# An mLSTM and band-attention trunk on one core: the values of all heads first, one loop of heads with seven products on 7 of 8 depth pairs, weight sums on GpSimd

## The chip, the core and the metric

The kernel runs on one core of a Trainium2 chip. TensorE (PE) multiplies, VectorE (DVE) and ScalarE (ACT) work on tiles, GpSimd (POOL) can add tiles too, and SyncE (SP) issues the DMAs. The metric is the device time of one execution in microseconds, as the median of several.

## The reference

Two layers run on x of 512 tokens by 2048 channels, in float32. The first is an mLSTM with 8 heads, the second a band attention with 16 heads over a shared K and V. Each layer is normalised, modulated by a projection of `c` (adaLN) and gated. The time goes into the large products:

```python
proj = h @ w_in                      # 512x2048 @ 2048x16400: q, k (8 x 256 each), v, o, z (8 x 512 each), gates
qk = silu(causal_conv(proj[..., :A_V0]))
ht = rmsnorm(mlstm_chunkwise(q, k, v, li, lf))
y = sigmoid(o) * ht * silu(z)
x = x + gate0 * rmsnorm(y @ w_out)   # 512x4096 @ 4096x2048
kv = hkv @ kv_w                      # 512x2048 @ 2048x4096, shared K and V
qz = h2 @ b_w_in                     # 512x2048 @ 2048x4096: queries and gate
out = x + gate1 * rmsnorm((attention(q, k, v) * silu(z)) @ b_w_out)
shift, scale, gate = split(silu(c) @ ada_w[l] + ada_b[l])   # 2048 -> 6144 for each layer, 4096 for K and V
```

## The kernel before

**Products in three passes.** Each float32 operand is split into a high part (a cast on ScalarE, line 181) and a low part (a subtraction on VectorE, line 182); `mm3` issues high x high, high x low and low x high on TensorE (line 223). The names `wr`, `wh` and `wl` are a weight as loaded, its high and its low part. `h` is the modulated input of a layer, in 16 depth tiles of 128 channels by 512 tokens.

**Eight or seven products.** A unit is two depth tiles by two output tiles of 128 columns by 512 tokens. In the plain form it takes four triples over 512 tokens, which count as eight of 256. `proj_s` computes some units in Strassen's manner, with seven triples over 256 tokens, into four PSUM tiles D, C, A and B; this needs four sums of the inputs (`h1s`, kept in SBUF) and three sums of the weights. VectorE makes the sums of the weights (`ws`, lines 206 to 208), and they are split in their turn (`wsh`, `wsl`). `HEAD_PAIRS = 5` of the 8 units of a pair of output tiles are done so in heads 5 to 7, `RAMP = [4, 5, 5, 5]` in the o and z pairs of head 4, none in heads 0 to 3, and `ATT_PAIRS = 7` of 8 in the queries of the attention.

**Stages.** The start makes `h1` block by block while it multiplies the rows that are ready: q, k, o and z of head 0 and q, k of head 1. Then heads 0 to 7 run in a loop: q and k with their convolution (line 529), the values in `proj_b` (`ps_v`), the scores between them, o and z, the weighted values, the normalisation, and the head's result to DRAM (`ysc`). Then come a_w_out (tiles `y`), the shared values and keys, the 16 attention heads, and b_w_out.

**The columns of adaLN.** The projection of `c` is done on VectorE: rows of the transposed weights are loaded (`ada`, 128x1024, 256 loads) and multiplied and summed into columns of `mod` (line 381). The first 64 loads belong to the start; `background(n)` issues the others in heads 0 to 4 and sums those that came before, held in program order.

**Order.** The tile scheduler orders each engine's instructions by priority; weights are prefetched under a high priority (`AHEAD = 300`). SP issues nearly all DMAs in one queue, and each waits there for its buffer. Raw weights have two buffers of 128x1024 and one more from a spare pool in the start, in heads 0 to 4 and in a_w_out.

Of the kernel before, what the change touches and what calls it, by code (L numbers as in the profile page):

```python
# [33 lines left out]
RAW_BUFS = 2  # L34
# [3 lines left out]
LEAD = [0, P, V0 // 2, V0 // 2 + P, O0, O0 + P]  # L38
LATER = [O0 + 2 * P, O0 + 3 * P] + [Z0 + i * P for i in range(4)]
LATER += [DK, DK + P, V0 // 2 + DK, V0 // 2 + DK + P]  # L40


KEY_PAIRS = [6, 7, 8, 8, 8, 8, 8, 8]
HEAD_PAIRS = 5
RAMP = [4, 5, 5, 5]
HALF = NH // 2
ATT_PAIRS = 7


def pair_pieces(f, merged=False):  # L50


    sk, nk = list(range(f)), list(range(f, KT // 2))
    n = len(nk)
    assert n <= f
    out = [([[a]], [b]) for a, b in zip(sk, nk)]
    return out + [([sk[i : i + 2]] if merged else [[k] for k in sk[i : i + 2]], []) for i in range(n, f, 2)]


def stream():  # L60
# [3 lines left out]
    def add(mat, kts, cs):  # L64
        out.append((mat, [(k, c, n) for k in kts for c, n in cs]))

    def tile_a(mat, col, kts=KT):
        for k in range(0, kts, 8):
            add(mat, range(k, k + 8), [(col, P)])

    def tile_b(mat, col, kts=KT):
        for k in range(0, kts, 2):
            add(mat, [k, k + 1], [(col, 512)])

    def tile_s(mat, c1, c2, f, merged=False):
        for sk, nk in pair_pieces(f, merged):
            blocks = [(2 * k + i, c, P) for ks in sk for i, c in ((0, c1), (0, c2), (1, c2), (1, c1)) for k in ks]
            out.append((mat, blocks + [(2 * k + i, c, P) for k in nk for i in range(2) for c in (c1, c2)]))

    for k0, k1 in BLOCKS:  # L80
        for k in range(k0, k1):
            add("a_w_in", [k], [(c, P) for c in LEAD])
        for c in LATER:
            add("a_w_in", range(k0, k1), [(c, P)])
    for h in range(NH):
        for c in (h * DK, V0 // 2 + h * DK):
            if 1 < h <= HALF:
                tile_a("a_w_in", c)
                tile_a("a_w_in", c + P)
            elif h > HALF:  # L90
                tile_s("a_w_in", c, c + P, HEAD_PAIRS)
        tile_b("a_w_in", V0 + h * DV)
        if h >= HALF:
            for i in range(4):
# [38 lines left out]
def hybrid_trunk(ctx, tc, xT, xN, c, adaT, cols, wst, wg, ext, kc, out):  # L133
# [131 lines left out]
    def proj_s(mat, xs, ss, f, z1, z2, name, pl, bufs, at={}, merged=False):  # L265
# [6 lines left out]
        for i, (sk, nk) in enumerate(pieces):  # L272
# [35 lines left out]
            if i:  # L308
                eight()
# [309 lines left out]
    for h in range(NH):  # L619
# [62 lines left out]
        if h:  # L682
            so = []
# [480 lines left out]
```

## Time and profile before

| | |
|---|---|
| median of 3 runs | 2831.57 us (2830.79 to 2834.91) |
| the profiled execution | 2835.43 us |
| its span, first to last instruction | 2833.7 us |
| TensorE busy | 2790.5 us, 98% of the span |
| VectorE, ScalarE busy | 2073.8 us (73%), 1337.3 us (47%) |
| moved by DMA | 524.61 MB, 185 GB/s in the mean |

All shares are of the profiled execution. A busy time counts an engine as busy from an instruction's start to its end; TensorE's matmuls overlap, so the cost of one is read from the distance between the starts of two. In a row by group stand the busy time of the group, the mean duration in ns, and the engine's idle time before its instructions with what ended it.

### The profile page before, as it was taken

What the parts mean: (1) busy time and instruction counts of PE and PEld (TensorE: products, weight loads), DVE (VectorE), ACT (ScalarE), POOL (GpSimd) and SP (SyncE); (2) the same over time, 40 slices, a digit from 0 to 9 for tenths busy, and PEclk for the clock granted to TensorE, in tenths of its full rate; (3) what the DMA queues carried; (4) which work ended last, traced back from release to release, by engine and by line L of the source; (5) the groups of instructions that cost most, each with busy time, mean ns of one, the idle gap of its engine ahead of it and who ended that gap; (6) DMA issues with size and microseconds to landing.
All of it is one profiled execution on the core that took longest, in us unless ns stands there. A gap on an engine that the chain in (4) does not pass through costs nothing.

```text
span 2833.7 us, 40698 instructions
## 1 busy us (share of the span) xinstructions
PE 2790.5 (98%) x15308; PEld 2423.1 (86%) x15308; DVE 2073.8 (73%) x3680; ACT 1337.3 (47%) x2005; POOL 0.2 (0%) x4
## 2 busy tenths in 40 slices
PE   7999999999999999999999999999999999999998
PEld 5887888888888989989888888888998899999886
DVE  7986978778688776857766445567885798999625
ACT  4244524234234554545545444468434466666523
POOL 0000000000000000000000000000000000000000
PEclk9999999999999999999999999999999999999999
DMA  8875787868774333323324666788435533333535
GB/s 307 303 249 178 233 309 244 298 231 277 263 244 134 101 108 97 108 93 105 108 90 145 217 197 223 240 273 274 163 127 176 175 123 127 129 113 125 197 133 167
DMA packets 177117, 524.61 MB, mean 185 GB/s; under 512 B 18788, under 2 KB 36228, under 8 KB 176408
## 3 DMA queue, kind: packets, MB, share of 16 engines
q1 hardware_dynamic: 176920, 522.01, 55.4%
q8 instruction: 120, 1.97, 0.3%
q14 instruction: 77, 0.63, 0.1%
HBM read 488.33 MB, written 38.85 MB: 186 GB/s over the span
## 4 chain that ended last, share of the span: by engine, by line
PE 86%; DVE 6%; DMA 4%; ACT 2%; issue 2%; SPq 0%; DVEq 0%; ACTq 0%
PE ps_y L223 17%; PE ps_v L223 10%; PE ps_o L223 5%; PE ps_z L223 5%; PE ps_azo L223 4%; PE ps_qk L223 4%; PE ps_kv L223 4%; PE ps_az L223 3%; PE ps_bzo L223 3%; PE ps_l L223 3%; PE ps_cz L223 3%; PE ps_dz L223 2%; PE ps_bz L223 2%; PE ps_s L223 2%; PE ps_czo L223 2%; PE ps_dzo L223 2%
## 5 line engine op out<-in xcount | busy, mean ns | idle before, releaser
L181 ACT CAST wh<-wr 128x1024 fp32r<-128x1024 f32 (+3 forms) x586 | 585.3, 1000 | 843.9 <-PE ps_y L223 203.7
L182 DVE TENSOR_TENSOR wl<-wr,wh 128x1024 fp32r<-128x1024 f32 (+3 forms) x586 | 679.1, 1161 | 410.1 <-ACT wh L181 407.6
L223 PE MATMUL ps_y<-wh,y 128*128 128x512 f32 x1536 | 475.9, 390 | 0.1
L223 PEld LDWEIGHTS ps_y<-wh,y 128*128 128x128 f32 x1536 | 288.2, 188 | 60.0 <-ACT wh L181 0.3
L223 PE MATMUL ps_v<-wh,h 128*128 128x512 f32 x1024 | 321.6, 390 | 0.1
L223 PE MATMUL ps_y<-wl,y 128*128 128x512 f32 x768 | 299.3, 390 | 0.4 <-DVE wl L182 0.2
L181 ACT CAST wsh<-ws 128x384 fp32r<-128x384 f32 (+1 forms) x253 | 138.4, 547 | 315.4 <-issue 122.2
L223 PEld LDWEIGHTS ps_v<-wh,h 128*128 128x128 f32 x1024 | 192.3, 188 | 40.2 <-issue 1.0
L182 DVE TENSOR_TENSOR wsl<-ws,wsh 128x384 fp32r<-128x384 f32 (+1 forms) x253 | 151.7, 600 | 97.7 <-ACT wsh L181 96.3
L223 PE MATMUL ps_v<-wl,h 128*128 128x512 f32 x512 | 199.8, 390 | 0.0
L381 DVE CUSTOM_DVE_ANT_0 ada<-ada,scB,mod 128x1024 f32<-128x1024 f32 x128 | 164.1, 1282 | 24.5 <-DMA ada<-in_adaT 23.2
L381 DVE CUSTOM_DVE_ANT_0 ada<-ada,scB,cl 128x1024 f32<-128x1024 f32 x128 | 164.0, 1282 | 24.1 <-DMA ada<-in_adaT 23.7
L223 PEld LDWEIGHTS ps_y<-wl,y 128*128 128x128 f32 x768 | 144.3, 188 | 31.0 <-DVE wl L182 1.5
L223 PE MATMUL ps_kv<-wh,hkv 128*128 128x512 f32 x512 | 159.4, 391 | 0.0
L206 DVE TENSOR_TENSOR ws<-wr 128x256 f32<-128x256 f32 (+1 forms) x253 | 112.5, 453 | 37.6 <-DMA wr<-in_wst 34.5
L223 PE MATMUL ps_qk<-h,wh 128*128 128x512 f32 x384 | 119.1, 390 | 0.0
L223 PE MATMUL ps_o<-h,wh 128*128 128x512 f32 x384 | 118.2, 389 | 0.0
L223 PE MATMUL ps_z<-h,wh 128*128 128x512 f32 x384 | 118.1, 389 | 0.0
L223 PEld LDWEIGHTS ps_v<-wl,h 128*128 128x128 f32 x512 | 96.2, 188 | 19.7 <-issue 0.9
L223 PEld LDWEIGHTS ps_kv<-wh,hkv 128*128 128x128 f32 x512 | 95.7, 188 | 19.4
L223 PE MATMUL ps_l<-h,wh 128*128 128x512 f32 x320 | 99.6, 392 | 0.9 <-ACT wh L181 0.5
L223 PE MATMUL ps_kv<-wl,hkv 128*128 128x512 f32 x256 | 99.9, 390 | 0.4 <-DVE wl L182 0.4
(385 smaller groups left out, 5918.8 us busy)
## 6 DMA issues: line engine op xcount, KB each, us to landing
wr<-in_wst SPq DMA_DIRECT2D x520, 512.0 KB, 3.6
ada<-in_adaT SPq DMA_DIRECT2D x256, 512.0 KB, 5.8
xt<-nsc SPq DMA_DIRECT2D x46, 256.0 KB, 3.7
yr<-ysc SPq DMA_DIRECT2D x16, 512.0 KB, 4.0
wr<-in_wst SPq DMA_DIRECT2D x30, 256.0 KB, 4.4
wr<-in_wst SPq DMA_DIRECT2D x16, 384.0 KB, 5.0
bsc<-in_ext SPq DMA_DIRECT2D x16, 320.0 KB, 6.4
xt<-in_xT SPq DMA_DIRECT2D x4, 1024.0 KB, 7.0
```

The costliest lines, as they stand in the source:

```text
L181: nc.scalar.copy(hi, src)
L182: nc.vector.tensor_tensor(lo, src, hi.bitcast(F32), op=ALU.subtract)
L206: nc.vector.tensor_tensor(t[:, : 2 * w], r[:, w : 3 * w], r[:, : 2 * w], op=ALU.subtract)
L223: nc.tensor.matmul(ps, a, b, start=start, stop=stop)
L381: pin(nc.vector.tensor_tensor_reduce(at, at, scB[:, j * D // 2 : (j + 1) * D // 2], 1.0, mod[:, i : i + 1] if j else col(CB + i), ALU.mult ...
```

## The change

- The values of all heads come first. The start multiplies the values of heads 0 to 3 (`FIRST = 4`) in place of q, k, o and z; heads 4 to 7 follow in a loop of `proj_b`. All are kept in DRAM (`vrow`) as float32 and fetched and split again in each head.
- One loop of heads does q, k, o and z of every head with seven products on 7 of 8 units (`HEAD_PAIRS = 7`); the attention takes 8 of 8. A unit's input sums for the second token half overwrite the high and low parts that are no longer used, so seven units' sums fit.
- The three sums of the weights are on GpSimd, with signs changed so that all are additions. A seven-product piece is one load of 128x512; it is staged one piece ahead, and its products are ordered so that the three that need no sum come first.
- One pool for the weights: raw tiles of 128x512, four of them, and three (`ws`) that hold sums, and raw tiles of plain pieces where no sums are needed; in a_w_out and the first shared values (`plain`) only four.
- The columns of adaLN are spread otherwise: 56 loads of 128x1024 among the values of heads 4 to 6; 104 quarters (128x512) in the loop of heads; 104 in a_w_out and the first shared values; 32 loads of 128x1024 in b_w_out. Small parts: the attention's bias has one buffer, `gates_out` works on four columns at a time.

```diff
-HEAD_PAIRS = 5
-RAMP = [4, 5, 5, 5]
-ATT_PAIRS = 7
+FIRST = 4
+HALF_KV = 12
+TICKS = (2, 3, 5, 6)
+HEAD_TILES = 26
+HEAD_PAIRS = 7
+ATT_PAIRS = 8
+    return [0, *range(f, UNITS), *range(1, f)]
...
-            raw = (spare[0] if own else wp).tile([P, 1024], F32, tag="raw", name=f"wr{i}", bufs=1 if own else RAW_BUFS)[:, :n]
-                nc.vector.tensor_tensor(t[:, : 2 * w], r[:, w : 3 * w], r[:, : 2 * w], op=ALU.subtract)
-                nc.vector.tensor_tensor(r[:, w : 2 * w], t[:, w : 2 * w], r[:, :w], op=ALU.add)
-                nc.vector.tensor_tensor(t[:, 2 * w :], r[:, 3 * w :], r[:, w : 2 * w], op=ALU.subtract)
...
+        tag = "ws" if spare and not plain[0] and fresh[0] % 7 > 3 else "raw"
+        return wp.tile([P, 512], F32, tag=tag, name=name, bufs=3 if tag == "ws" else 4)
...
+            if not seven:
+                for c in range(0, n, 512):
+                    raw = rawtile(f"wr{i}_{c}", blocks[0][2] == 512)
+                    nc.sync.dma_start(raw, src[:, c : c + 512])
+                    cast = split(hi[:, c : c + 512], lo[:, c : c + 512], raw)
+            else:
+                raw = rawtile(f"wr{i}", False)
+                nc.sync.dma_start(raw, src)
+                t = wp.tile([P, 512], F32, tag="ws", name=f"ws{i}")
+                nc.gpsimd.tensor_tensor(
+                    t[:, : 2 * w].rearrange("p (a b) -> p a b", a=2), raw[:, : 2 * w].rearrange("p (a b) -> p a b", a=2),
+                    raw[:, 3 * w :].unsqueeze(1).to_broadcast([P, 2, w]), op=ALU.add,
+                )
+                nc.gpsimd.tensor_tensor(t[:, 2 * w : 3 * w], t[:, :w], raw[:, w : 2 * w], op=ALU.add)
+                nc.gpsimd.tensor_tensor(t[:, 3 * w :], t[:, 2 * w : 3 * w], raw[:, 2 * w : 3 * w], op=ALU.add)
+                cast = split(hi[:, : 3 * w], lo[:, : 3 * w], raw[:, : 3 * w])
+        staged.append((mat, hi, lo, t, cast))
+    def wpiece(want):
+        early = t is not None or AHEAD_ALL
+        if early and wpos[0] < len(order):
+            stage()
+        if t is not None:
+            with tc.high_priority(ahead[0]):
+                split(hi[:, 384:896], lo[:, 384:896], t)
...
+            raws = [(D, h0, 0, x0[:, :, h0]), (A, h0, 2, x1[:, :, h0]), (B, h0, 1, s[3])]
+            sums = [(D, h1_, 5, s[1]), (C, h0, 4, s[2]), (C, h1_, 3, s[0]), (A, h1_, 6, x1[:, :, h1_])]
+            steps = raws + sums
...
+    for h in range(FIRST, NH):
+        at = {k: lambda k=k: background((3, 2)[k // 2 % 2]) for k in range(0, KT, 2)}
+        proj_b("a_w_in", lambda k: h1[k], pv, at=at)
+                keep_rows(h, m, pv[m])
...
+        hooks = [{6: score[0]}, {1: score[1], 4: score[2], 7: score[3]}, {1: fetch[0], 3: fetch[1], 5: fetch[2], 7: fetch[3]}, {}]
+            o, sz = pair(O0 + h * DV + i * P, f"zo{h}_{i}", hooks[i], TICKS if i else ())
...
-    rows(0, range(4), y_tile)
+    rows(0, range(4), y_tile, {k: late_quarter for k in range(8, 32, 2)})
+            add_at(at, {k: late_quarter for k in range(2, 32, 2)})
```

In the order VectorE's instructions stood like this in a seven-product head before, at the end of its first q pair (`ws` are the weight sums, `wsl` their low parts, `zq` the results of the pair):

```order
L182 TENSOR_TENSOR wl_9938<-wr_9931,wh_9937 128x1024
L206 TENSOR_TENSOR ws_0_9980<-wr_9978 128x256
L182 TENSOR_TENSOR wsl_0_9942<-ws_0_9933,wsh_0_9941 128x384
L207 TENSOR_TENSOR wr_9978<-ws_0_9980,wr_9978 128x128
L208 TENSOR_TENSOR ws_0_9980<-wr_9978 128x128
L314 TENSOR_TENSOR zq_0_1_9643<-zq_0_0_9642,ps_dzq_0_9644 128x256
```

At the end of such a pair after the change, VectorE has:

```order
L180 TENSOR_TENSOR wl_7210<-ws_7213,wh_7209 128x512
L794 TENSOR_TENSOR zo_2_0_6322<-zo_2_0_6322,dd_6899 128x512
L794 TENSOR_TENSOR zo_3_0_6616<-zo_3_0_6616,dd_6899 128x512
L180 TENSOR_TENSOR wl_7274<-wr_0_7275,wh_7273 128x512
L316 TENSOR_TENSOR zq_0_1_6983<-zq_0_0_6982,ps_dzq_0_6984 128x256
```

The three additions are gone from it, and a unit's split is now in two instructions, 384 raw columns and 512 of sums. They stand on GpSimd, in the same head:

```order
L216 TENSOR_TENSOR ws_7114<-wr_7112 128x256
L220 TENSOR_TENSOR ws_7114<-ws_7114,wr_7112 128x128
L221 TENSOR_TENSOR ws_7114<-ws_7114,wr_7112 128x128
L740 TENSOR_TENSOR nmd_7548<-nm_7547,maskd 128x512
L216 TENSOR_TENSOR ws_7147<-wr_7145 128x256
```

Each addition after the first reads what the one before it wrote; besides these, only the head's mask sum (`nmd`) is there.

SP's queue before, among the values of an early head, where loads for adaLN and weights alternate:

```order
L199 DMA wr_5234<-in_wst 128x1024
L377 DMA ada_1_4911<-in_adaT 128x1024
L377 DMA ada_0_4913<-in_adaT 128x1024
L199 DMA wr_5276<-in_wst 128x1024
L377 DMA ada_1_4915<-in_adaT 128x1024
L377 DMA ada_0_4990<-in_adaT 128x1024
```

After, among the values of head 4:

```order
L209 DMA wr_512_2521<-in_wst 128x512
L209 DMA wr_0_2575<-in_wst 128x512
L380 DMA ada_0_2264<-in_adaT 128x1024
L380 DMA ada_1_2302<-in_adaT 128x1024
L380 DMA ada_0_2304<-in_adaT 128x1024
L209 DMA wr_512_2579<-in_wst 128x512
```

Two or three loads of `ada` stand between the two halves of one weight piece, and this goes on for three heads of values in a row. In a_w_out SP had weights and the row of the gate (`ssum`) before:

```order
L199 DMA wr_14497<-in_wst 128x1024
L199 DMA wr_14515<-in_wst 128x1024
L779 DMA ssum<-ggd 128x512
L199 DMA wr_14533<-in_wst 128x1024
L199 DMA wr_14551<-in_wst 128x1024
```

At the same row of the gate it has after the change:

```order
L597 DMA qa_73_19629<-in_adaT 128x512
L835 DMA ssum<-ggd 128x512
L209 DMA wr_0_19633<-in_wst 128x512
L209 DMA wr_512_19637<-in_wst 128x512
L597 DMA qa_74_19654<-in_adaT 128x512
```

Each piece is two loads now, and a quarter of adaLN (`qa`) follows it.

621 lines of the change are left out of this document (329 added, 292 removed).

## The prediction

> **What bounds the kernel now.** I read the page first, then the sums by stage, then what TensorE waited for, and last the instructions of one pair of products in order of time. The page gives the span and the busy times:
>
> ```profile
> span 2833.7 us, 40698 instructions
> PE 2790.5 (98%) x15308; PEld 2423.1 (86%) x15308; DVE 2073.8 (73%) x3680; ACT 1337.3 (47%) x2005; POOL 0.2 (0%) x4
> PE 86%; DVE 6%; DMA 4%; ACT 2%; issue 2%; SPq 0%; DVEq 0%; ACTq 0%
> ```
>
> TensorE is busy for 98%, and the chain that ended last runs over it for 86%. GpSimd does nothing. By stage (columns: from and to, length, busy time of PE, PEld, DVE, ACT and POOL with counts, clock, DMA share, GB/s):
>
> ```profile
> 0.00:216.00 216.00, 199.85 (x827) 158.47 (x828) 182.84 (x314) 83.08 (x128) 0.20 (x4) 0.99 0.81 285
> 330.00:420.00 90.00, 88.85 (x395) 73.39 (x394) 70.51 (x104) 28.27 (x38) 0.00 (x0) 1.00 0.91 315
> 992.00:1173.00 181.00, 181.00 (x1115) 163.39 (x1114) 128.36 (x240) 89.06 (x125) 0.00 (x0) 1.00 0.32 102
> 1173.00:1354.00 181.00, 181.00 (x1115) 163.40 (x1114) 128.76 (x240) 89.23 (x125) 0.00 (x0) 1.00 0.31 102
> 1535.00:1888.00 353.00, 351.00 (x1566) 290.33 (x1566) 188.23 (x207) 166.78 (x233) 0.00 (x0) 1.00 0.69 221
> 1888.00:1981.00 93.00, 92.55 (x426) 75.65 (x425) 71.22 (x115) 74.74 (x129) 0.00 (x0) 1.00 0.86 281
> 2237.00:2640.00 403.00, 400.05 (x3010) 382.04 (x3008) 360.59 (x954) 255.51 (x480) 0.00 (x0) 1.00 0.40 128
> 2640.00:2834.00 194.00, 182.84 (x812) 150.18 (x812) 86.15 (x118) 68.75 (x107) 0.00 (x0) 0.98 0.50 167
> ```
>
> The rows are the start; a piece of the early heads, with the densest DMA that I found (315 GB/s at a share of 0.91); heads 5 and 6; a_w_out; the first shared values; the attention; and the tail. In heads 5 and 6 TensorE has no gap at all. The attention shows that it keeps going (400.05 of 403) even where Vector is busy 360.59 of 403, which is 89%. TensorE's longest waits, in total, times, longest:
>
> ```profile
> PE ps_lead L223 <- ACT h L358: 7.8, 4, 3.4
> PE ps_x L223 <- DVE xsq L428: 4.1, 1, 4.1
> PE ps_czo L223 <- DVE v L182: 3.3, 1, 3.3
> ```
>
> These are small, so the time follows what TensorE must do, and that is where the change can gain. One unit (two depth tiles by two output tiles) stands here in both forms, eight products from 1001.56 and seven from 1004.30 to 1006.82:
>
> ```profile
> 1001.56 0.63 PE L223 MATMUL ps_azq<-h,wh 128*128 128x512 f32 x2
> ...
> 1004.30 0.40 PE L223 MATMUL ps_dzq<-h1s,wh 128*128 128x256 f32 x2
> ...
> 1006.82 0.40 PE L223 MATMUL ps_dzq<-h1s,wh 128*128 128x256 f32 x2
> ```
>
> Eight products take 2.74 us, or 0.685 us for each of the four triples; seven take 2.52 us. A unit turned from eight to seven is worth 0.22 us, not the eighth (0.34 us) that the count of products suggests.
>
> **The change part by part.** *Units.* After it, 8 heads have 6 pairs of tiles with 7 seven-product units each, 336. Before, heads 5 to 7 have 6 pairs of 5, and head 4 has 4+5+5+5, together 109. The attention goes from 7 to 8 in 16 heads. That is 227 + 16 = 243 units, and 243 x 0.22 = 53.5 us less on TensorE. The values' products (64 triples per head, 43.8 us) move to the front with their cost unchanged, and so does the number of products in the start. From the 181 us of head 5 or 6, taking away 43.8 for the values and 12 x 0.22 for twelve more units leaves 134.6 us for one turn of the new loop of heads.
>
> *Vector in a head.* The rows (shape, count, busy, mean ns of one):
>
> ```profile
> L182 DVE TENSOR_TENSOR wl<-wr,wh 128x1024 fp32r<-128x1024 f32 x520 | 635.3, 1223 | 404.0 <-ACT wh L181 401.6 <-PE ps_cz L223 0.8
> L182 DVE TENSOR_TENSOR wsl<-ws,wsh 128x384 fp32r<-128x384 f32 x224 | 124.0, 554 | 76.2 <-ACT wsh L181 74.9
> L182 DVE TENSOR_TENSOR wl<-wr,wh 128x512 fp32r<-128x512 f32 x30 | 20.6, 689 | 0.8 <-ACT wh L181 0.8
> L206 DVE TENSOR_TENSOR ws<-wr 128x256 f32<-128x256 f32 x224 | 92.6, 422 | 36.5 <-DMA wr<-in_wst 33.8
> L207 DVE TENSOR_TENSOR wr<-ws,wr 128x128 f32<-128x128 f32 x224 | 61.7, 284 | 1.5
> L208 DVE TENSOR_TENSOR ws<-wr 128x128 f32<-128x128 f32 x224 | 63.0, 288 | 2.7
> L381 DVE CUSTOM_DVE_ANT_0 ada<-ada,scB,mod 128x1024 f32<-128x1024 f32 x128 | 164.1, 1282 | 24.5 <-DMA ada<-in_adaT 23.2
> L529 DVE SCALAR_TENSOR_TENSOR cv<-zq,cl,cv 128x511 f32<-128x511 f32 x12 | 8.7, 748 | 0.0
> ```
>
> Head 5 has 30 seven-product units, so 30 x (0.422 + 0.284 + 0.288) = 29.8 us of weight sums leave Vector. Its splits are now 32 x 1.223 + 30 x 0.554 = 55.8 us and will be 42 x (0.554 + 0.689) + 12 x 0.689 = 60.5 us. Thirteen quarters of ada columns come in, each a little over half of 1.282 us, 9 us. So 128.4 - 29.8 + 4.7 + 9 = 112 us in 134.6, or 83%: below the 89% at which the attention still runs without gaps. In the attention itself 8 x 0.994 us of sums leave Vector per head.
>
> *GpSimd.* The trace shows no arithmetic on it. From below, Vector's own rows for the same three adds bound a unit: 0.994 us. From above, I take the slowest pass over 512 columns in the trace, Vector's reciprocal:
>
> ```profile
> L736 DVE RECIPROCAL dd<-dd 128x512 f32<-128x512 f32 x8 | 26.8, 3352 | 5.0 <-ACT dd L735 5.0
> ```
>
> 3.35 us is more than the 2.52 us of a unit and would make GpSimd the bound. I go near the lower row, as it is the same operation, and take 1.0 to 1.5 us. The adds run one unit ahead, so a lag below a unit is hidden by the unit in progress; without that cover each unit would wait 1 us or more. The Trainium skill, "GPSIMD Engine Reference", section "Performance versus the Vector engine", gives 1.96 times Vector's time for such an add; by that the three would take about 1.9 us (an estimate), which still fits in a unit, and the sum would not change. No run so far shows it. I put 1 us per head, 8 us, for units that come late behind bursts on Vector (evacuation, scores, quarters). It can't be below nothing, since TensorE has no gap there now; its upper end is the first rival.
>
> *Head values first.* Heads 4 to 7 now stand in a row with 20, 20 and 16 ada loads of 512 KB. The DMA rows (KB each, us to landing):
>
> ```profile
> wr<-in_wst SPq DMA_DIRECT2D x520, 512.0 KB, 3.6
> ada<-in_adaT SPq DMA_DIRECT2D x256, 512.0 KB, 5.8
> wr<-in_wst SPq DMA_DIRECT2D x30, 256.0 KB, 4.4
> ```
>
> Heads 4 and 5 move 20 x 512 KB of ada, 4096 KB of weights and 1024 KB of kept values each, 15.7 MB in 43.8 us. That asks for 359 GB/s, and the densest stretch showed 315, at which it takes 50 us. SP issues weights and ada loads in one queue, so an ada load that waits for its buffer holds back the weights behind it. I add 6 us for each of the two heads, 12 us; from 0 (the weights' seven buffers bridge it) to 27 us (at the start's 285 GB/s over all three heads' 45 MB).
>
> *Start.* The same products and bytes; the next block's rows of h1 are now made among the products of this one, where before TensorE waited for them (the 7.8 us row). I take 5 us off; from 10 off to 10 on, as one ada buffer is gone.
>
> *a_w_out and first values.* 102 quarters of 256 KB join 353 us at 221 GB/s: 78 + 26.7 = 104.7 MB, 297 GB/s, below 315. ScalarE's casts:
>
> ```profile
> L181 ACT CAST wh<-wr 128x1024 fp32r<-128x1024 f32 x520 | 545.6, 1050 | 739.0 <-PE ps_y L223 203.7 <-PE ps_v L223 92.2 <-PE ps_z L223 90.7
> L181 ACT CAST wh<-wr 128x512 fp32r<-128x512 f32 x30 | 18.5, 621 | 56.3 <-PE ps_l L223 28.6 <-PE ps_lead L223 20.4 <-DMA wr<-in_wst 5.3
> ```
>
> The raw weights' buffers shrink from three of 512 KB to four of 256 KB, and the halves of a_w_out use one every 1.37 us. A buffer's turn is landing 4.4 (the 256 KB row), cast 0.621, and split 0.689, 5.7 us against 4 x 1.37 = 5.48. That is 4% of 446 us, 18 us, if each landing takes 4.4; with 3.6 it is nothing. I take 8; 2 us off is the lower end, as TensorE idles 2 us there.
>
> *Tail and joints.* 32 ada loads (16.8 MB) move into the tail, which goes from 167 to 253 GB/s; at the joint of values and heads the last sums must be split, like the 3.3 us wait at the joint now. 3 us; from 5 off to 8 on. The changed signs, the pools and the single bias buffer keep the count of operations or load a head ahead, nothing.
>
> The sum: 2833.7 - 53.5 - 5 + 12 + 8 + 8 + 3 = 2806.2 us of span. The profiled execution took 2835.43, 1.7 more than its span, and the median of the three runs, 2831.57, is 3.9 below it: **2804 us**.
>
> **The rivals.** *Vector and GpSimd exclude each other (slower).* Vector's instructions with two operands from SBUF in a head: splits 60.5, quarters 9, convolutions 12 x 0.748 = 9, and some 20 more of 512 columns x 0.689 = 14, together 92 us. If GpSimd's adds can't run beside these, 42 x t must fit in the 134.6 - 92 = 42 us left, so it decides from t = 1.0 us, just Vector's own pace. Not all of an instruction need block: 512 columns more cost 1.223 - 0.689 = 0.534 us, so about three quarters of each is streaming, 70 us, and then the point is 1.5 us. For t between 1.3 and 2 us the excess goes from nothing or 13 us (the two points) to 19 or 42 us per head; I take 10, 80 us in eight heads, and leave out the 8 us above: 2876 us. The attention has room (8 units in 403/16 = 25 us a head). Nothing in the trace speaks for or against, as GpSimd is idle. The Trainium skill, "SBUF — State Buffer", section "Who interferes with whom", has this rule: a Vector instruction with two SBUF inputs contends with a GpSimd instruction that reads SBUF, and the second to issue fully blocks. No run so far shows it.
>
> *Loads bind (about no change).* Values-first costs its 27 us, a_w_out its 18 us, and the tail its 8: 30 us above my sum, 2834 us. For it: the 0.91 share at 315 GB/s, and four small buffers. Against: the weights' waits now are mostly on TensorE (Vector's splits wait for the casts, 404.0 us, and most of the casts' 739.0 us of idle time ends with TensorE).
>
> *No new wait shows (faster still).* Without the 12, 8, 8 and 3: 2773 us. For it: everything new runs a unit ahead. That the change doesn't do what it says I leave out, since both forms of the unit stand in the trace.
>
> **How the numbers follow.** About 0.2% (5.7 us) is what a measurement of this kernel can tell from no change. My forecast, 2785 to 2825 us, has 0.46; no new wait 0.16; loads bind 0.13, with 0.03 faster, 0.06 within, 0.04 slower; exclusion 0.25, with 0.01 within and 0.24 slower. Faster 0.65, same 0.07, slower 0.28. The lower end is the sum with each term at its low bound (2763 in span, 2761 in time), of which I leave out a little: 2765. The upper end takes in most of the exclusion up to 2885; about 0.12 lies above and 0.03 below.
>
> **What would show it.** Right: one turn of the loop of heads takes 134 to 136 us with Vector at 83%, GpSimd 1.0 to 1.5 us a unit, the values of heads 4 and 5 about 50 us each, a_w_out near 360 us. Exclusion: Vector's splits last longer than 0.554 and 0.689 us or GpSimd's adds stretch, and TensorE waits for the lower halves from GpSimd's sums in the heads, with turns of 140 us or more. Loads bind: casts wait for the raw weights in a_w_out. The prediction is wrong if a turn differs from 135 us by more than 5 us, or if TensorE's time for a unit isn't 2.52 us.

## The result, and the profile after

The changed kernel takes 2921.93 us (median of four runs, 2916.62 to 2924.36), the kernel before 2833.24 us (2830.79 to 2835.18) beside it. The ratio is 1.0311, with a 95% interval of 1.0293 to 1.0329: 3.1% slower, where 2804 us was forecast. The span is 2922.6 us.

The page of the changed kernel opens so:

```profile
span 2922.6 us, 50260 instructions
PE 2800.4 (96%) x17498; PEld 2506.5 (86%) x17498; DVE 2389.5 (82%) x4049; ACT 1560.9 (53%) x2878; POOL 1232.8 (42%) x1615
```

TensorE has gaps now, 122 us where 43 stood before, though a busy share of 96% hides that at first sight. By stage (columns as in the prediction's table):

```profile
0.00:219.00 219.00, 198.94 (x824) 158.72 (x825) 185.51 (x317) 73.31 (x117) 0.20 (x4) 0.99 0.88 312
219.00:427.00 208.00, 193.83 (x811) 153.09 (x811) 148.21 (x218) 59.95 (x108) 33.10 (x34) 0.96 0.67 227
427.00:1561.00 1134.00, 1104.21 (x8194) 1049.14 (x8193) 1063.91 (x1609) 696.85 (x1208) 798.31 (x1011) 0.99 0.44 135
1561.00:1947.00 386.00, 368.99 (x1584) 293.81 (x1582) 259.80 (x503) 181.10 (x335) 0.00 (x0) 0.99 0.81 264
1947.00:2056.00 109.00, 97.86 (x418) 76.36 (x417) 77.02 (x153) 77.17 (x162) 2.46 (x4) 0.97 0.84 274
2056.00:2233.00 177.00, 169.05 (x1316) 164.20 (x1315) 137.51 (x206) 84.19 (x161) 130.91 (x180) 0.96 0.46 147
2233.00:2321.00 88.00, 88.00 (x393) 72.83 (x392) 58.41 (x110) 45.48 (x82) 10.58 (x15) 1.00 0.60 193
2321.00:2717.00 396.00, 395.48 (x3157) 387.85 (x3156) 331.29 (x713) 270.02 (x561) 257.24 (x369) 1.00 0.44 132
2717.00:2922.00 205.00, 184.03 (x816) 150.50 (x814) 127.83 (x226) 72.78 (x150) 0.00 (x0) 0.98 0.72 244
```

The rows are the start, the values of heads 4 to 7, the loop of heads, a_w_out, the first shared values, the keys, the other shared values, the attention and the tail. Where TensorE's own time is named below, it is the number of products times the usual distance between their starts in that stage. For one turn of the loop of heads it is 134.3 us, where 134.6 was forecast, but the turns take 142; Vector is busy 1064 of the loop's 1134 us, 94%. a_w_out takes 386 us where it took 353 (357 when counted from its first product, as after the change), the first values 109 where they took 93, the keys 177 after 168, the tail 205 after 194. The attention alone gained, 396 after 403.

What TensorE waited for in the loop of heads (us in total, times, longest), and Vector's and GpSimd's groups of weights:

```profile
PE ps_czq L241 <- DVE zq L316: 12.9, 8, 2.0
PE ps_azo L241 <- DVE zo L319: 6.1, 19, 0.7
```

```profile
L180 DVE TENSOR_TENSOR wl<-ws,wh 128x512 fp32r<-128x512 f32 x525 | 477.0, 909 | 21.6 <-ACT wh L179 21.5
L180 DVE TENSOR_TENSOR wl<-wr,wh 128x384 fp32r<-128x384 f32 x525 | 356.9, 680 | 95.2 <-ACT wh L179 94.4
L216 POOL TENSOR_TENSOR ws<-wr 128x256 f32<-128x256 f32 x525 | 497.6, 948 | 943.1 <-ACT v L937 506.7 <-DVE wl L180 292.8 <-DMA wr<-in_wst 135.6
L220 POOL TENSOR_TENSOR ws<-ws,wr 128x128 f32<-128x128 f32 x525 | 360.2, 686 | 41.2
L221 POOL TENSOR_TENSOR ws<-ws,wr 128x128 f32<-128x128 f32 x525 | 346.4, 660 | 41.2
```

The waits are for Vector's evacuation of a pair's results, not for the weights' sums. Both of Vector's splits last longer than the 689 and 554 ns forecast. Sorted by what GpSimd did meanwhile, the split of 512 columns has a mean of 684 ns where no add ran beside it and about 1000 ns where one ran for most of it; an add of 128 columns has 460 ns alone and some 680 beside Vector. Vector's evacuations, with one operand in PSUM, don't change: 682 ns without an add beside, 684 with.

Which of the two starts first decides who is held up. Four instructions of GpSimd and Vector in order of time (start, duration):

```profile
458.28 0.99 POOL L216 TENSOR_TENSOR ws<-wr 128x256 f32<-128x256 f32 x1 [2.36 <-DVE wl L180]
458.60 1.22 DVE L180 TENSOR_TENSOR wl<-ws,wh 128x512 fp32r<-128x512 f32 x1
459.35 0.79 POOL L220 TENSOR_TENSOR ws<-ws,wr 128x128 f32<-128x128 f32 x1
459.74 0.94 DVE L547 SCALAR_TENSOR_TENSOR cv<-zq,cl,cv 128x509 f32<-128x509 f32 x1
```

The split starts while the first add runs, and ends 0.55 us after it. The second add starts while the split runs, and ends 0.32 us after it. The convolution ends 0.54 us after the second add. In the loop of heads 256 splits of 512 columns started while an add ran: they took 1.01 us in the mean and ended 0.55 us after the add in the median. The 44 beside which an add only started later took 0.68 us, as long as alone. So the one that starts second waits for the first to end, and only some 0.13 us of its own time (0.68 less 0.55) pass beside the other.

### The profile page after: what moved, and what is told of

Read it like the earlier page. It is cut to its first block, busy times and chain, and to the rows that moved or that the text cites. A ratio compares the mean times of both kernels' runs of the same rounds, so it can differ in the third digit from the quotient of the medians.

```text
span 2922.6 us, 50260 instructions
## 1 busy us (share of the span) xinstructions
PE 2800.4 (96%) x17498; PEld 2506.5 (86%) x17498; DVE 2389.5 (82%) x4049; ACT 1560.9 (53%) x2878; POOL 1232.8 (42%) x1615
## 5 line engine op out<-in xcount | busy, mean ns | idle before, releaser
L179 ACT CAST wh<-wr 128x512 fp32r<-128x512 f32 (+1 forms) x1104 | 609.3, 567 | 822.6 <-DMA wr<-in_wst 150.7
L180 DVE TENSOR_TENSOR wl<-wr,wh 128x512 fp32r<-128x512 f32 (+1 forms) x1104 | 752.7, 697 | 257.7 <-ACT wh L179 253.6
L216 POOL TENSOR_TENSOR ws<-wr 128x256 f32<-128x256 f32 x525 | 497.6, 948 | 943.1 <-ACT v L937 506.7
L180 DVE TENSOR_TENSOR wl<-ws,wh 128x512 fp32r<-128x512 f32 x525 | 477.0, 909 | 21.6 <-ACT wh L179 21.5
L179 ACT CAST wh<-ws 128x512 fp32r<-128x512 f32 x525 | 324.1, 617 | 112.4 <-POOL ws L221 60.3
L220 POOL TENSOR_TENSOR ws<-ws,wr 128x128 f32<-128x128 f32 x525 | 360.2, 686 | 41.2
L221 POOL TENSOR_TENSOR ws<-ws,wr 128x128 f32<-128x128 f32 x525 | 346.4, 660 | 41.2
L241 PE MATMUL ps_azo<-h,wh 128*128 128x256 f32 (+1 forms) x1024 | 219.3, 299 | 6.8 <-DVE zo L319 6.1
L241 PEld LDWEIGHTS ps_azo<-h,wh 128*128 128x128 f32 x1024 | 161.5, 191 | 14.9 <-DVE zo L319 11.1
L241 PE MATMUL ps_czo<-h1s,wh 128*128 128x256 f32 x896 | 172.1, 284 | 1.9 <-DVE zo L316 1.8
L241 PE MATMUL ps_v<-wh,h 128*128 128x512 f32 x512 | 164.2, 401 | 3.4 <-ACT wh L179 3.3
```

The costliest lines, as they stand in the source:

```text
L179: cast = nc.scalar.copy(hi, src)
L180: nc.vector.tensor_tensor(lo, src, hi.bitcast(F32), op=ALU.subtract)
L216: nc.gpsimd.tensor_tensor(t[:, : 2 * w].rearrange("p (a b) -> p a b", a=2), raw[:, : 2 * w].rearrange("p (a b) -> p a b", a=2), raw[:, 3 * ...
L220: nc.gpsimd.tensor_tensor(t[:, 2 * w : 3 * w], t[:, :w], raw[:, w : 2 * w], op=ALU.add)
L221: nc.gpsimd.tensor_tensor(t[:, 3 * w :], t[:, 2 * w : 3 * w], raw[:, 2 * w : 3 * w], op=ALU.add)
L241: nc.tensor.matmul(ps, a, b, start=start, stop=stop)
```

## The experiments: the heads

Theory A: GpSimd's adds and Vector's instructions with two SBUF operands hold each other up. Rival B: Vector has too much of its own at the joints between pairs. Rival C: the chain load, three adds, split is too long.

**No sums.** The three adds go, and the raw piece is split in the place of their result:

```diff
-                raw = rawtile(f"wr{i}", False)
+                raw = rawtile(f"wr{i}")
...
-                t = wp.tile([P, 512], F32, tag="ws", name=f"ws{i}")
...
+                t = raw
```

> The changed kernel without the three adds on GpSimd per unit: the raw piece is split in the place of the sums, so this part of the computation is left out; Vector and ScalarE do as many splits as before, and the seven raw tiles of 256 KB are shared by all pieces. Theory A (GpSimd's adds and Vector's instructions with two operands in SBUF hold each other up, and the late Vector is what TensorE waits for at the joints between pairs): the 512-column split falls from 909 ns to about 690, Vector's busy time per turn of the head loop from 134 us to about 110, the turn from 142 us to 134.5-136.5, the run to about 2860-2878. Rival B (Vector has too much of its own in bursts at the joints, GpSimd or not): the turn stays at 140 or more, the run at 2905 or more. Rival C (the chain of three adds between load and split is too long, whatever it does to Vector): as A, so this run does not tell A from C.

Measured: 2855.32 us, ratio 1.0072 (1.0056 to 1.0087). One turn, without the sums:

```profile
826.80:961.50 134.70, 134.70 (x1029) 130.26 (x1028) 108.93 (x203) 87.61 (x152) 1.29 (x1) 1.00 0.46 138
```

and the same turn in the changed kernel:

```profile
853.00:994.50 141.50, 138.34 (x1027) 131.50 (x1025) 133.75 (x203) 87.37 (x151) 101.21 (x127) 0.99 0.43 131
```

With the same 203 instructions Vector is busy 108.9 us in place of 133.8, and TensorE has no gap. The loop of heads goes from 1134 to 1075 us, the keys from 177 to 170. B falls. But even without the sums the kernel is 0.7% slower than the kernel before, so the heads are only a part of the story.

**Unread sums.** The three adds write a tile that nothing reads (`u = wp.tile(...)`), and the raw piece is split.

> The changed kernel with the same three adds on GpSimd, but nobody reads their result: the raw piece is split in their place (this leaves the sums out of the computation). GpSimd has the same work, but no product waits for it. Theory A (the engines hold each other up): the turn stays at 140-142.5 us, the 512-column split at about 900 ns, the run at 2905-2925. Rival C (the chain of adds is too long): turn about 135 us, run about 2865. Rival B (Vector alone): as A here, 2905-2925; it is told from A by the run without the adds.

Measured: 2920.74 us, ratio 1.0304 (1.0286 to 1.0321). The turn:

```profile
845.20:986.00 140.80, 137.44 (x1028) 130.64 (x1027) 133.70 (x203) 86.89 (x152) 100.78 (x127) 1.00 0.46 132
```

No product waits for GpSimd here, and the loop of heads still takes 1126 us. C is at most 9 us of 59; A is shown. (The run without sums also had seven raw tiles for these pieces in place of four, but in the turn with unread sums no cast waits for a raw weight to land, so the tiles are not the difference.)

**Sums on Vector.** `nc.gpsimd` becomes `nc.vector` in the three adds.

> The changed kernel with the three adds on Vector in place of GpSimd, nothing left out. Alone on Vector they would take about 0.42 + 0.29 + 0.29 = 1.0 us per unit, 42 us per turn. Theory A: Vector without the hindrance needs about 110 us per turn and with the adds about 152, which is more than TensorE's 134, so the turn becomes 150-156 us and the run 2985-3035: the move to GpSimd did bring something, only less than forecast. Rival C (the chain of adds on GpSimd was the cost): the turn falls or stays, run 2922 or below. Rival B: as A, or longer still, over 3035.

Measured: 2922.5 us, ratio 1.0313 (1.0296 to 1.0331): the changed kernel's time within a microsecond. The turn:

```profile
843.60:985.90 142.30, 138.63 (x1029) 132.21 (x1028) 137.93 (x330) 92.08 (x157) 1.78 (x1) 0.99 0.44 132
```

My expectation of 150 to 156 us missed, since I priced the adds by their durations. (C's number, 2922 or below, nearly came out, but the unread sums leave C at most 9 us.) Two rows of its order of time show why (start, duration):

```profile
902.95 0.42 DVE L216 TENSOR_TENSOR ws<-wr 128x256 f32<-128x256 f32 x1
903.29 0.74 DVE L547 SCALAR_TENSOR_TENSOR cv<-zq,cl,cv 128x511 f32<-128x511 f32 x1
```

The next instruction starts 0.34 us after a 0.42 us one. By the busy times, 42 trios cost Vector 137.9 - 108.9 = 29.0 us when it makes them itself, 0.69 us each, and 133.8 - 108.9 = 24.8 us, 0.59 us each, when GpSimd makes them. The move took 4 of 29 us off Vector.

**The kernel before with its sums on GpSimd**, one part of the change alone (lines 206 to 208 on `nc.gpsimd`).

> The kernel before with its three subtractions and additions of the weights on GpSimd in place of Vector, and nothing else changed (heads 4 to 7 and the 16 attention heads have them). Vector is the tighter engine only in the attention there (360.6 of 403 us), and TensorE lost only 6.8 us in it. Theory A: Vector's two-operand splits stretch where GpSimd adds, but Vector has room, so the run is 2826-2842, no more than 0.4% either way. Rival B (Vector's own load is what costs): 2 to 8 us faster, 2824-2830. Rival C (the chain on GpSimd is too long, with only one piece of lead): TensorE waits for sums in every unit, 15 us slower or more, 2847 or above.

Measured: 2891.79 us, ratio 1.0203 (1.0188 to 1.0218). A's and B's times missed. It is the rival C that comes nearest, in the attention, which goes from 406 to 459 us; heads 5 to 7, where Vector is busy 62%, keep their 181 us each. ScalarE's longest wait in the attention with the sums on GpSimd, the same before, and TensorE's waits with them on GpSimd:

```profile
ACT wh L181 <- POOL wr L207: 152.3, 61, 4.3
```

```profile
ACT wh L181 <- DVE wr L207: 39.7, 33, 2.7
```

```profile
PE ps_t L1015 <- DVE pt L182: 14.9, 15, 1.4
PE ps_az L223 <- DVE z L317: 10.2, 13, 0.8
```

In this kernel the second sum overwrites a column of the raw weights that the cast reads, so ScalarE waits for GpSimd, Vector's split for ScalarE, and the evacuations stand behind the split. The changed kernel's casts of the raw columns don't wait for a sum, so this cost is the old kernel's own.

The heads of this run show something else. 180 us of them in the kernel before, and with the sums on GpSimd:

```profile
1083.00:1263.00 180.00, 180.00 (x1108) 162.49 (x1107) 126.92 (x238) 88.34 (x123) 0.00 (x0) 1.00 0.31 103
```

```profile
1083.00:1263.00 180.00, 180.00 (x1106) 162.22 (x1105) 109.56 (x150) 89.06 (x124) 68.80 (x90) 1.00 0.31 103
```

Vector wins 17 us by the move, of about 20 that some 29 trios cost it at 0.69 us each (an estimate), where the changed kernel won 4 of 29. GpSimd runs beside a busy Vector for 41 of its 70 us here, and for 95 of 101 us in a turn of the changed kernel. So the worth of the move depends on how often the adds meet a Vector that is at work.

**Five units, on GpSimd and on Vector** (`HEAD_PAIRS = 5`, the second with the adds on `nc.vector`).

> The changed kernel with seven products on five of eight units in the heads in place of seven: 30 units with sums per turn in place of 42, the other 12 plain. TensorE's products then take 134.3 + 12 x 0.22 = 136.9 us per turn. Theory A (GpSimd's adds and Vector hold each other up): the hindrance falls with the adds, by 12/42 or, since Vector then has room at the joints, by more; the loss per turn falls from 7.6 us to 1-4 us, the turn is 138-141 us and the run 2895-2918. Rival B (what Vector does at the joints anyway): the loss stays at 7.6, the turn becomes 144.5 and the run 2943.

> The changed kernel with seven products on five of eight units in the heads and with the three adds on Vector in place of GpSimd, nothing left out. TensorE's products take 136.9 us per turn. From the runs with the adds on GpSimd, on Vector and left out, Vector is busy 134.0, 137.7 and 108.9 us per turn with 42 units, so an add trio costs Vector 0.69 us where it makes them itself and 0.60 us where GpSimd does. With 30 units on Vector that is 108.9 + 30 x 0.69 = 129.5 us, under TensorE's 136.9. Theory A: turn 137.5-139.5, heads together 1100-1118 us (on GpSimd with five units: 1117.6), the run at 2885-2908. Rival (on Vector the bursts at the joints cost more than on GpSimd): turn 140.5 or more, the run at 2915 or more.

Measured: 2907.78 us, ratio 1.0267 (1.0252 to 1.0282), turns of 140 us; and 2901.51 us, 1.0233 (1.0217 to 1.0248), turns of 138.2 to 140.1. The loop of heads takes 1118 and 1112 us. Fewer sums help by more than the plain units cost, as A has it, and Vector makes them at no higher price than GpSimd.

## The experiments: the other stages

**Three waits eased.** TensorE's waits among the values of the changed kernel:

```profile
PE ps_v L241 <- DVE wl L180: 5.4, 4, 3.2
PE ps_at L539 <- DVE ssum L530: 5.2, 1, 5.2
PE ps_v L241 <- ACT wh L179: 3.3, 1, 3.3
```

```diff
+        if h == FIRST + 1:
+            add_at(at, {4: gates_turned})
...
-        nc.gpsimd.tensor_tensor(r0[:, a], r0[:, a], r0[:, b], op=ALU.subtract)
...
-        gates_out(1, 4 * g, 4 * g + 4)
...
+                add_at(hooks, {14: lambda g=g: gates_row(g)})
```

`gates_turned` is the last five lines of `gates`, the transposes and their copy, and `gates_row` the call taken out of `gates_end`; of the four subtractions on GpSimd in `head_sums` the first is shown.

> The changed kernel with three places eased: the transposes of the gates' columns come a head later than the chain on Vector that makes them; the four subtractions per unit on GpSimd in the input sums beside the last head of values are left out (so this part of the computation is left out); in b_w_out the transposes of the gates' rows come some pieces after their sums. Theory A (the three are separate waits of 5, 8 and 10 us, and GpSimd hinders Vector in the last head of values too): values of heads 4 to 7 in 194-200 us in place of 207.6, the tail 10 us shorter, the run at 2895-2905. Rival (the last head of values waits because Vector has the sums and splits of all seven units in 50 us, GpSimd or not): values 200-204, the run at 2903-2909. Rival (the waits only change places): 2915 or more.

Measured: 2908.75 us, ratio 1.027 (1.0255 to 1.0286). The values take 191.7 us in place of 207.9: the gates' transposes and GpSimd beside the last head of values are the cause, and Vector's sums there are not too many. The two were not taken apart. The tail did not gain (212 us): the gate's row then came late for the evacuation (7.1 us at one place), so that wait only changed places.

**Seven raw tiles, no quarters, another queue.** In a_w_out ScalarE's casts waited for the raw weights in the changed kernel, as forecast for *Loads bind* (columns as for TensorE's waits):

```profile
ACT wh L179 <- DMA wr<-in_wst: 119.8, 75, 4.9
```

```diff
-    plain[0] = True
+    plain[0] = False
```

> The changed kernel, with seven raw tiles of 256 KB in place of four in a_w_out and the first shared values (three of them shared with the quarters of adaLN). The changed kernel took 386 us and 109 us there, of which TensorE's products by their usual distances are 354 and 92. Theory A (four raw tiles hold too few loads in flight): a_w_out 354-362, first values 92-97, the run at 2872-2888. Rival Q (the quarters of adaLN, one load and one sum on Vector in between, are what delays the weights in SP's queue): with the quarters still there and now in the same three tiles, a_w_out 375 or more, the run at 2905-2925. Rival D (the DMA engines are full at 265 GB/s): no change, 2918-2925.

Measured: 3013.08 us, ratio 1.0639 (1.0623 to 1.0654), a_w_out 493 us. The quarters then rotate through the same tiles as the weights and wait in SP's queue for a weight to be used up; the second row is the changed kernel's own:

```profile
SPq L597 <- DMA wr<-in_wst: 62.9, 25, 4.4
```

```profile
SPq L597 <- DVE mod L586: 20.8, 37, 2.9
```

So this run says what a shared tile costs in one queue, and nothing on the number of tiles. Leaving the quarters out (`late_quarter` only sets its columns to zero):

> The changed kernel without the 104 quarters of adaLN in a_w_out and the first shared values (their columns are set to zero, so this part of the computation is left out). Theory A (four raw tiles are too few): the raw tiles are as few as before, so most of the loss stays: a_w_out 370-382, first values 98-107, the run at 2895-2915. Rival Q (the quarters' loads and sums delay the weights): a_w_out 354-360, first values 92-96, the run at 2872-2882. Rival D (bandwidth): 27 MB fewer at 265 GB/s would be over 100 us, so all of the loss goes as in Q, and the DMA rate falls to about 220 GB/s; the run with seven raw tiles tells D from Q.

Measured: 2878.28 us, ratio 1.016 (1.0135 to 1.0186); a_w_out 362 us, first values 99. That is Q's time for the run, and A misses. The quarters are 34 of the 45 to 49 us that the two stages lost (45 with a_w_out before at 357 us). The late loads on another queue (`eng.dma_start` with `nc.gpsimd` in `late_quarter` and `last_gates`):

> The changed kernel with nothing left out; the 104 late quarters of adaLN (in a_w_out and the first shared values) and the 32 last loads of adaLN (in b_w_out) are issued by GpSimd's DMA queue in place of SP's, with the same tiles, bytes and sums. Theory Q (a quarter that waits in SP's queue for its tile holds up the weights behind it): a_w_out falls from 386 us to 362-368, the first values from 109 to 98-102, b_w_out's stage from 206 to 197-203, the run to 2878-2892. Rival V (the sums of the quarters on Vector delay the weights' splits): the sums are all still there, a_w_out 380 or more, the run at 2912 or above. Rival D (DMA bandwidth): as V, the same bytes in the same time.

Measured: 2944.37 us, ratio 1.0382 (1.0367 to 1.0397); a_w_out 407 us, first values 100, tail 223. Theory Q, that a quarter in SP's queue is what holds the weights up, falls for a_w_out and the tail; the bounds of V and D came out. Why these two stages became slower than in the changed kernel is not shown.

**Loads alone, sums alone, later sums.**

> The changed kernel with the late quarters of adaLN loaded in a_w_out and the first shared values but not summed (their columns are set to zero, so this part of the computation is left out). Three theories stand for the 24 us that a_w_out, and 10 us that the first values, gain without the quarters. Theory L (the quarters share the DMA engines with the weights, so a weight lands later than four raw tiles cover): all loads are still there, a_w_out 378-390, first values 105-110, the run at 2910-2925. Theory H (a sum that is held in program order waits on Vector for its quarter, with the weights' splits behind it): a_w_out 360-366, first values 98-101, the run at 2878-2888. Theory V (86 us of sums are simply too much on Vector): as H.

> The changed kernel without the loads of the late quarters; the 104 sums are made, but from the row of silu(c) that lies in SBUF (so this part of the computation gives other numbers). Theory L (loads): a_w_out 360-368, first values 98-101, the run at 2878-2890. Theory H (waiting sums): the sums wait for nothing, the same numbers as L. Theory V (the sums' work on Vector): a_w_out 378-390, first values 105-110, the run at 2910-2925.

> The changed kernel, nothing left out; in a_w_out and the first shared values a quarter is summed one hook later, so that two are on their way and the sum finds its quarter landed. Theory H (Vector waits in its queue for the quarter): the 29 us of Vector's waits for quarters go, a_w_out 362-372, the run at 2888-2905. Theory L (weights land late because of the quarters' loads): no change, a_w_out 380-390, the run at 2915-2925. Theory V: no change either.

Measured: loads alone 2915.51 us, ratio 1.0278 (1.026 to 1.0295); sums alone 2884.58, 1.0162 (1.0141 to 1.0183); later sums 2935.68, 1.0352 (1.0336 to 1.0367). a_w_out without quarters, with their loads alone, with their sums alone, in this order:

```profile
1559.00:1921.00 362.00, 356.35 (x1583) 293.17 (x1583) 200.38 (x323) 183.19 (x350) 0.00 (x0) 1.00 0.65 217
```

```profile
1560.00:1937.00 377.00, 366.58 (x1584) 293.53 (x1583) 198.18 (x313) 181.19 (x336) 0.00 (x0) 0.99 0.83 269
```

```profile
1557.00:1923.00 366.00, 358.80 (x1587) 294.81 (x1586) 266.84 (x527) 184.78 (x350) 0.00 (x0) 1.00 0.68 217
```

The loads cost 15 us, the sums 4, both together 24: so theory V falls, and H as the main cause, since the run with the loads alone has no sums that could wait. L's times came out in both runs, to 1 us. ScalarE's wait for raw weights in a_w_out shows the same, without quarters and with their loads alone (119.8 us in the changed kernel, 51.2 with the sums alone):

```profile
ACT wh L179 <- DMA wr<-in_wst: 31.3, 25, 3.1
```

```profile
ACT wh L179 <- DMA wr<-in_wst: 119.2, 81, 4.8
```

The loads by themselves make the weights land too late for the casts. Later sums, which should have helped if H were the cause, made a_w_out 398 us, above L's range too, and Vector's wait for quarters 40 us in place of 28.

**Own tiles, with the rest that helped, and with the queue besides.**

```diff
-    plain[0] = True
+    plain[0] = False
...
-    tp = tst.enter_context(pool("t2", bufs=5, side="right"))
+    tp = tst.enter_context(pool("t2", bufs=3, side="right"))
...
-        quarter(rest, lambda name: wp.tile([P, S], F32, tag="ws", name=name))
+        quarter(rest, lambda name: rp.tile([P, S], F32, tag="qa", name=name, bufs=2))
```

> The changed kernel, nothing left out, with seven raw tiles for the weights in a_w_out and the first shared values, and two tiles of their own for the late quarters (room for them comes from the row tiles, three in place of five, which may cost a few us where rows are turned). All bytes and sums are as in the changed kernel. Theory L, sharpened (the loads share the DMA engines, so a weight lands later, and four raw tiles of 256 KB don't cover that): the pieces ahead of the row turning go at TensorE's pace, 43.5 us for an eighth of the products of a_w_out in place of 45-49; a_w_out 362-374, first values 98-106, the run at 2885-2905. Theory B (the DMA engines carry no more): a_w_out 382 or more, the run at 2915 or more, whatever the number of tiles.

> The changed kernel, nothing left out, with the edits that helped so far: five units of seven products in the heads and all sums of weights and inputs on Vector (2901.5 with the first alone), the transposes of the gates' columns a head later and the input sums beside the last head of values on Vector (12 us in the values, 5 in the keys), and the tiles of the run with own tiles. Theory L: 2901 - 17 - 25 = 2859, 2845-2875. Theory B: 2880-2892. Both stay above the kernel before.

> The run with all that helped and own tiles, nothing left out, and the late quarters of adaLN issued by GpSimd's queue besides; b_w_out's loads stay on SP. So the weights have seven raw tiles, and no weight stands behind a quarter in SP's queue. In the run with own tiles the quarters, now in two tiles, held SP's queue 77 us (20.8 us in the changed kernel), and a_w_out took 396-400 us; where they did not hold it, an eighth with 14 or 15 quarters took 43.5 us, TensorE's pace. Theory L with Q (both are needed: enough raw tiles, and no quarter ahead of the weights in their queue): a_w_out 365-382 with a few us of that for the row tiles, the run at 2888-2910. Theory B (the DMA engines carry no more on the whole), or a rival in which Vector's wait for a quarter is what holds the weights: a_w_out 392 or more, the run at 2916 or more.

Measured: 2948.22 us, ratio 1.0385 (1.0365 to 1.0404), a_w_out 396; 2925.45, 1.0312 (1.0294 to 1.033), a_w_out 400; 2922.49, 1.032 (1.0303 to 1.0338), a_w_out 422. In the first two the first values took 118 and 116 us and the keys 189 and 185, longer than in the changed kernel (109 and 177). In the last, with the same three row tiles, they took 99 and 177, so that this loss goes with the quarters in SP's queue. The first holds SP's queue at the quarters, the last frees it and holds Vector instead:

```profile
SPq L597 <- DVE mod L586: 75.8, 69, 3.6
```

```profile
DVE qa L589 <- DMA qa<-in_adaT: 89.6, 65, 4.9
```

A quarter's sum is held in program order on Vector, so while it waits for its load, the weights' splits wait behind it. In the first of these runs ScalarE's wait for raw weights is down from 119.8 us:

```profile
ACT wh L179 <- DMA wr<-in_wst: 20.2, 22, 3.3
```

But Vector's wait for quarters is up from 28 to 72 us there. So the tiles cured the wait that L names, and H's took its place. Two eighths of a_w_out's products in the second of these runs, with the sums of 29 quarters beside them, ran without a gap:

```profile
1622.00:1709.00 87.00, 87.00 (x385) 71.88 (x384) 62.78 (x125) 39.34 (x70) 0.00 (x0) 1.00 0.86 273
```

They moved 273 GB/s, so the DMA engines aren't simply full at the 264 of the changed kernel, as theory B has it, though B's numbers for the whole stage came out in the first and the last run; in the second both theories' times missed, and L's did in all three, with or without Q. What stays open is whether the same 27 MB can be had at no cost over the whole stage: the other orders of the same bytes took 396 us to 493, and only leaving the loads out recovered it. No run gave the quarters tiles of their own and summed them late enough for Vector not to wait.

**All that helped, before own tiles were tried** (five or six units, sums of weights and inputs on Vector, gates' transposes later, late loads on GpSimd's queue).

> The changed kernel, nothing left out, with what the runs so far suggest: five units of seven products in the heads, all sums of weights and inputs on Vector, the late loads of adaLN on GpSimd's queue, the transposes of the gates' columns a head later. If the costs add: 2922 - 30 (heads 1134 to 1104) - 22 (a_w_out) - 8 (first values) - 5 (b_w_out) - 5 (gates) - 5 (fewer sums beside the last head of values) = 2847, 2838-2860. That is still over the kernel before (2832): the plain units and what is left of the values' stage and of the late loads' waits cost more than the one loop of heads brings. Rival (the waits hide one another, so that the gains do not add): 2870 or more.

> As the run with all changes and five units, but six units of seven products in the heads, nothing left out. TensorE's products take 135.6 us per turn, Vector 108.9 + 36 x 0.69 = 133.7 us, 99% of that. Theory A (Vector at 94% and over makes the joints wait, whoever does the adds): turn 138-140.5, no gain over five units, the run within 6 us of that with five, 2840-2862. Rival (Vector's share does not matter on its own): turn 136-137.5, 10-14 us faster than with five units.

Measured: 2912.47 us, ratio 1.0269 (1.0255 to 1.0283), and 2925.88, 1.0314 (1.0298 to 1.033). The values (193 and 190 us) and the keys (167 and 166) gained as hoped, even with the input sums on Vector; the other queue lost it again in a_w_out (405 both) and the tail (223 and 228), so that the sum of the gains, 2847 us, missed by 65. Six units bring turns of 136 to 147 us, no gain over five at 139, as theory A has it for a Vector at 99% of TensorE's time; but the run is 13 us slower than with five, where A allowed 6. No version beat the kernel before.

## Why the prediction was wrong

**Units: right.** TensorE's own time for a turn is 134.3 us (forecast 134.6), and without the sums a turn takes 134.7. The attention gained 7 us where 3.5 were forecast.

**Vector in a head: the step that failed.** "112 in 134.6, or 83%" priced Vector's rows as they stood beside an idle GpSimd. That number was right for such a Vector (108.9 us in the run without sums) and wrong for this kernel, 133.8 us, since each trio on GpSimd costs Vector 0.59 us. At 94% in place of 83% its evacuations come late at the joints, and TensorE waits for them. The 8 us put there became 60 (1134 less 8 x 134.3). GpSimd's own price, 1.0 to 1.5 us a unit, was off too: 948 + 686 + 660 ns make 2.29 us, 1.66 alone (735 + 460 + 462).

**The rival of exclusion** had the mechanism: stretched splits and adds, turns over 140 us, 60 us in all where 80 were put. Its formula with three quarters of an instruction blocked gives 42 x 1.66 - 64.6 = 5 us a turn for the adds' time alone (an estimate from rows of the runs); 7.5 were measured. Its place was slightly different: TensorE waits for evacuations queued behind the splits, not for the lower halves from the sums. I gave it 0.25, because the trace had no row of GpSimd. The Trainium skill, "SBUF — State Buffer", section "Who interferes with whom", says that the second of two such instructions fully blocks. The runs agree on which instructions are hit (two SBUF operands, not one in PSUM) and on who waits: a split that starts while an add runs ends 0.55 us after that add, and one that starts first keeps its 0.68 us. The Trainium skill, "GPSIMD Engine Reference", section "Performance versus the Vector engine", gives 1.96 times Vector's time, for an add of 2048 columns; alone the adds here took 1.74 times (735 against 422 ns) and 1.6 times (460 against 286).

**Head values first: half the size, and mostly another mechanism.** 12 us were put for loads in heads 4 and 5. The stage lost 24 (208 us against 184 of its own, which has 9 for the gates' products), but 16 of them went with the gates' transposes and GpSimd beside the last head, so that 8 are left for the loads at most.

**a_w_out and first values: mis-sized, 8 us forecast, 45 to 49 measured.** The formula for a buffer's turn had the weights' own loads only. What it lacked was the quarters: 34 us, of which their loads are the larger part (21 us alone, against 4 for the sums alone). What the remaining 11 to 15 us are is open. That 297 GB/s lay below the densest stretch's 315 was no proof of room.

**Start and tail: also mis-sized.** The start took 219 us in place of 211. The tail took 11 us more, not 3; TensorE's longest wait there:

```profile
PE ps_gg L614 <- DVE ggate L612: 10.3, 4, 5.1
```

The transposes of the gates' rows stand behind sums of the last 32 loads. The keys' 9 us were not forecast; without the weights' sums nearly 8 of them are gone.

## What to carry to other kernels

Work that moves from Vector to GpSimd is to be priced by what Vector then takes for everything else that reads two operands from SBUF: here Vector won 4 of 29 us, because the adds nearly always met a Vector at work, and 17 of about 20 in the heads of the kernel before, where they met it less. How long GpSimd itself took hardly mattered to TensorE. Vector at 94% of the loop made TensorE wait at its joints, so an engine's share must be reckoned with the new neighbour running. Loads pushed into a stage that streams weights can delay the weights even where the DMA engines have been seen to move more: with the loads alone, ScalarE's wait for weights in a_w_out went from 31 to 119 us. Tiles of their own moved that wait to Vector's queue and did not remove it.

## What the runs showed of the hardware that was not expected

- Of a GpSimd add and a Vector instruction with both operands in SBUF, the one that starts second waits for the first: 256 splits of 512 columns that started while an add ran ended 0.55 us after it, and 44 that started first kept their 0.68 us.
- A duration is not a price: on Vector the next instruction starts some 80 ns before the last one ends (0.34 us after the start of a 0.42 us add), so three adds of 0.99 us by duration cost 0.69.
- The same loads issued by GpSimd's queue in place of SP's took a_w_out from 386 to 407 us and the tail from 206 to 223.
- The granted clock fell to 0.96 in the values and 0.97 in the first values, stages in which TensorE had gaps, and stayed at 1.00 in the attention, which had next to none. Gaps alone don't set it: in the tail TensorE was busy 90% of the time at 0.98, in the values 93% at 0.96.
